# First projection section in contraction order, last pair's down weights in two parts, seventeen weight buffers in a diffusion transformer block

## The chip, the core and the metric

The kernel runs on one core of a Trainium2 chip. The metric is the device time of one execution in microseconds (us). Engines are named as in the profile: PE (TensorE, matrix products), DVE (VectorE), ACT (ScalarE), POOL (GpSimd) and SP (SyncE, which here only issues transfers). Before the change three executions took 1332.74, 1338.11 and 1338.48 us, median 1338.11.

## The reference

One block for 512 tokens of width 1024, with 256 context tokens, all in f32. A condition vector gives six vectors of shift, scale and gate (`adaln`). The mixer is a gated linear recurrence with four heads in both directions, started from states of the context, beside a short convolution. The second half is a mixture of 16 experts in which each expert takes its 64 best tokens.

```python
sh1, sc1, g1, sh2, sc2, g2 = adaln(c, w_ada, b_ada)       # silu(c) @ w_ada + b_ada, split in 6
hc = modulate(rms_norm(ctx, norm_mix), csh1, csc1)         # the same from c_ctx
zf_f, zf_b, i_c = split(hc @ w_in[:, 512:2048])
s_f, s_b = hgrn2_context_states(zf_f, zf_b, i_c, ...)
hx = modulate(rms_norm(x, norm_mix), sh1, sc1)
q, zf_f, zf_b, i, g, gate_b, gate_c, v = split(hx @ w_in)  # eight sections of 512 columns
x = x + g1 * (concat(o_hgrn, gate_b * dwconv3(gate_c * v)) @ w_out)
h = modulate(rms_norm(x, norm_ffn), sh2, sc2)
aff = softmax(h @ w_router); gate, idx = top_k(aff.T, 64)
hid = silu(xs @ w_gate) * (xs @ w_up)                      # xs = h[idx], per expert 64 x 1024
x = x + g2 * scatter_add(idx, gate * (hid @ w_down))       # w_*: 16 experts, 1024 x 2048
out = rms_norm(x, norm_final)
```

## The kernel before

**Front.** The first 71 us compute shift and scale of the first norm and section 1 of `w_in` (the forward gates). A unit of `w_ada` is 1024 rows by 256 columns, 1 MB (`ada_unit`, L183): eight products into four column groups of PE, summed by two transposes and a reduction on DVE (`ada_cols`, L193). A loop over `j` (four steps of two of the eight contraction blocks `k`) loads a scale and a shift unit, modulates blocks `2j` and `2j+1` of tokens (`xnT`) and context (`cnT`), each split into a high and a low part, and adds their products for two of the section's four column groups (`products`, L262). Each f32 product is made of three fast ones: high by high, high by low and low by high. `px_f` and `pc_f` are the sums for the 512 tokens and 256 context tokens. The other two groups follow in `project_T(1, 1)`.

Sections 2, 4 and 3 and the four heads' context states (`context_state`, L369, both directions) follow to 185 us. The remaining columns of `w_ada` are multiplied by the condition on DVE meanwhile (`ada_sum`, L529: one multiply and seven multiply-adds of 128x256 per unit, each vector in four units) and summed over partitions on PE (`ada_r`, `ada_c`); the four units for the second gate `g2b` stand in the head stage among sections 6, 7, 0 and 5 (`sections`, L623). The router's weights `wr` are loaded by POOL after `g2b`'s bias and scaled on DVE (L615). This tile lies in memory that held the context's activations. The head stage ends at 311 us; output projection, router and the choice of tokens fill the time to about 390 us.

**Experts.** Pairs of experts are worked through: gate and up weights in 1 MB tiles (8 KB rows) into four sums `gu` (L897), transposes, and the down product `y` (L954). `scatter` (L927) brings the rows back to their tokens by a product with a 0/1 matrix. SP issues all weight loads in program order into a ring of 4 + 12 buffers (`NA`, `NB`), through `stream` (L60) at line 64. A load waits until the buffer's previous tile has been used.

**Last pair.** The down product of the last two experts goes by column parts 0 to 512, 512 to 768 and 768 to 1024. Each part is finished (L977: gate, scatter, squares for the final norm) while the next one is multiplied; tiles of the last part come in pieces of 256 KB. After the last part each of the four token blocks has its own chain of square, sum, reciprocal root, scaling and output transfer.

The order within an engine is set by a scheduler that follows program order and priorities (`high_priority`), as far as operands and banks allow.

## Time and profile before

| | us |
|---|---|
| three executions | 1332.74, 1338.11, 1338.48 |
| profiled execution, its own time | 1336.76 |
| its span, first to last instruction | 1334.8 |
| first section, to the first `ada_r` product | 0 to 71.4 |
| sections 2, 4, 3 and context states | to 185 |
| head stage | to 311 |
| projection, router, choice of tokens | to about 390 |
| experts | to 1281 |
| last down product and end | to 1334.8 |

The profile is of one execution. PE's clock granted over the span is 0.983 of full speed. A timeline row gives start, duration, engine, line, operation, output and inputs, and in brackets the idle time before it with what ended it. Matmuls overlap their neighbours, so the distance of two starts is the pace, not the duration. SPq is the queue of SP's transfers.

### The profile page before, as it was taken

Reading aid. Unit: us, or ns where it says so; the run is one execution under the profiler, and the core shown is the slowest. Engines: PE = TensorE matmul, PEld = TensorE weight load, DVE = VectorE, ACT = ScalarE, POOL = GpSimd, SP = SyncE. Lnnn points to the kernel's source line nnn. Section 1 sums busy time; section 2 is a strip of 40 time slices with the busy share of each in tenths; the row PEclk is TensorE's granted clock in tenths of the full one; section 3 lists DMA queues with packets and bytes.
Section 4 is the critical chain, followed back from the end, with each engine's and each line's share of the span. In section 5 each row is a group of like instructions: output and inputs, shape, how many; then the busy total and the mean of one; then the engine's idle time right before and its main releaser. Section 6 shows DMA issues by size and latency. Waiting matters only on the chain.

```text
span 1334.8 us, 15459 instructions
## 1 busy us (share of the span) xinstructions
PE 1264.9 (95%) x6374; PEld 692.5 (52%) x6374; DVE 420.5 (32%) x969; ACT 245.0 (18%) x494; POOL 43.6 (3%) x51
## 2 busy tenths in 40 slices
PE   5999989998969999999999999999999999999996
PEld 3788978776844443444444344344434434443433
DVE  5776467986451112112101211211021121102114
ACT  5633444334211200010000001000000100000002
POOL 1000022140000000000000000000000000000000
PEclk9999989998979999999999999999999999999998
DMA  9868223316389989999999999999999999999996
GB/s 328 267 201 261 96 82 96 127 64 234 143 330 407 358 347 426 426 427 427 427 426 426 425 427 427 427 427 426 425 427 427 427 427 426 427 425 427 426 385 215
DMA packets 112082, 458.85 MB, mean 344 GB/s; under 512 B 7310, under 2 KB 56571, under 8 KB 64907
## 3 DMA queue, kind: packets, MB, share of 16 engines
q1 hardware_dynamic: 110832, 454.06, 84.6%
q0 software_dynamic: 992, 3.74, 0.8%
q8 instruction: 50, 0.82, 0.2%
q14 instruction: 22, 0.17, 0.0%
q10 hardware_dynamic: 186, 0.06, 0.0%
HBM read 455.73 MB, written 2.10 MB: 343 GB/s over the span
## 4 chain that ended last, share of the span: by engine, by line
PE 87%; DVE 7%; ACT 3%; DMA 2%; issue 1%; POOL 0%; DVEq 0%; ACTq 0%; POOLq 0%; SPq 0%
PE gu L897 37%; PE y L954 17%; PE pg L855 5%; PE po L929 3%; PE px L265 3%; PE px L266 3%; PE px L270 3%; PE ht L912 2%; PE y L1009 1%; PE wo L710 1%; PE wo L711 1%; PE wo L712 1%; DMA wd<-in_w_down 1%; PE pi L335 1%; PE pi L333 1%
## 5 line engine op out<-in xcount | busy, mean ns | idle before, releaser
L897 PE MATMUL gu<-wg,xs 128*64 128x512 f32 x1024 | 461.7, 599 | 0.7 <-ACT gs L907 0.7
L897 PE MATMUL gu<-wu,xs 128*64 128x512 f32 x1024 | 460.7, 599 | 0.0
L954 PE MATMUL y<-wd,hid 128*64 128x512 f32 x896 | 239.2, 598 | 0.0
L897 PEld LDWEIGHTS gu<-wg,xs 128*64 128x64 f32 x1024 | 128.7, 136 | 158.1 <-issue 154.3
L897 PEld LDWEIGHTS gu<-wu,xs 128*64 128x64 f32 x1024 | 128.7, 136 | 123.1 <-issue 122.5
L907 DVE COPY gs<-gu 128x512 f32<-128x512 f32 x32 | 22.0, 691 | 389.8 <-PE gu L897 389.8
L954 PEld LDWEIGHTS y<-wd,hid 128*64 128x64 f32 x896 | 82.2, 136 | 120.1 <-issue 113.8
L907 ACT COPY gs<-gu 128x512 f32<-128x512 f32 x32 | 18.7, 587 | 455.1 <-PE gu L897 455.1
L265 PE MATMUL px<-h_hi,whi 128*128 128x512 f32 x208 | 85.1, 409 | 0.0
L270 PE MATMUL px<-h_hi,wlo 128*128 128x512 f32 x208 | 84.0, 404 | 0.0
L855 PEld LDWEIGHTS pg<-ohr,x 128*128 128x128 f32 x512 | 62.4, 195 | 40.6 <-issue 38.9
L266 PE MATMUL px<-h_lo,whi 128*128 128x512 f32 x208 | 83.4, 401 | 0.0
L855 PE MATMUL pg<-ohr,x 128*128 128x128 f32 x512 | 71.8, 289 | 1.5 <-DVE ohr L847 1.5
L861 DVE TENSOR_SCALAR xs<-pg,a,b 128x128 f32<-128x128 f32 x32 | 13.1, 410 | 149.1 <-PE pg L855 149.1
L258 DVE TENSOR_TENSOR wlo<-wi,whi 128x1024 fp32r<-128x1024 f32 x32 | 42.3, 1326 | 34.4 <-ACT whi L257 34.3
L923 DVE SCALAR_TENSOR_TENSOR yt<-y,gate,g2b 128x512 f32<-128x512 f32 (+1 forms) x17 | 12.2, 719 | 128.8 <-PE y L954 108.6
L535 DVE SCALAR_TENSOR_TENSOR adas<-wa,cs,adas 128x256 f32<-128x256 f32 x112 | 51.5, 492 | 1.2
L858 ACT ACTIVATE xs<-pg,b,a 128x128 f32<-128x128 f32 x32 | 14.6, 457 | 199.7 <-PE pg L855 199.7
L929 PE MATMUL po<-yhl,g 128*128 128x512 f32 (+1 forms) x136 | 41.7, 418 | 7.5 <-ACT yhl L924 7.0
L265 PEld LDWEIGHTS px<-h_hi,whi 128*128 128x128 f32 x208 | 40.2, 193 | 8.4 <-issue 0.4
L966 DVE TENSOR_TENSOR acc<-acc,po 128x512 f32<-128x512 f32 x56 | 36.0, 684 | 26.8 <-PE po L929 26.8
L929 PEld LDWEIGHTS po<-yhl,g 128*128 128x128 f32 x136 | 22.4, 189 | 42.1 <-ACT yhl L924 14.3
...
## 6 DMA issues: line engine op xcount, KB each, us to landing
wg<-in_w_gate SPq DMA_DIRECT2D x128, 1024.0 KB, 17.4
wu<-in_w_up SPq DMA_DIRECT2D x128, 1024.0 KB, 18.1
wd<-in_w_down SPq DMA_DIRECT2D x124, 1024.0 KB, 19.5
...
```

The source lines that it names most:

```text
L258: dve.tensor_tensor(lo, v, hi.bitcast(F32), op=ALU.subtract)
L265: mm(px, hi[:, k], h_hi[:, k], start=f, stop=False)
L266: mm(px, hi[:, k], h_lo[:, k], start=False, stop=False)
L270: mm(px, lo[:, k], h_hi[:, k], start=False, stop=l)
L535: dve.scalar_tensor_tensor(acc, t[:, k * 256:(k + 1) * 256], cs[:, k, 0:1], acc, op0=ALU.mult, op1=ALU.add)
L855: mm(pg[:, :P], x1[:, tb, k * P:(k + 1) * P], ohr[:, tb], start=tb == 0, stop=tb == NT - 1)
L897: mm(gu[n][i * CAP:(i + 1) * CAP], xs[:, k, ssl], w[:, n * 512:(n + 1) * 512], start=k == 0, stop=k == KD - 1, skip_group_check=True)
L907: (act.copy if n % 2 else dve.tensor_copy)(to, fr)
L912: pe.transpose(pt[:, i * P:(i + 1) * P], gs[:, f * P:(f + 1) * P], ident)
L929: mm(po, g[:, tb * P:(tb + 1) * P], yhl[:, i, nsl], start=first and i == 0, stop=i == 1)
L954: mm(y[n][i * CAP:(i + 1) * CAP], hid[:, i, f], wd[i][:, s, n * 512:(n + 1) * 512], start=f == 0, stop=f == DFF // P - 1, skip_group_check ...
L966: dve.tensor_tensor(acc[tb][:, nsl], acc[tb][:, nsl], po, op=ALU.add)
```

## The change

The ring of buffers in `ring_b` grows from 12 to 13. Memory for it comes from sharing: one tile (`shared`) holds the small constants and later the experts' gathered tokens `xs`, and one (`pool_a`) the working rows of the top-k and later the one-hot `ohr`.

The first section is computed for all four column groups at once, in order of the contraction: `k` 0 to 3 for the tokens, then for the context, then `k` 4 to 7. `w_ada`'s units become 512 wide (two tiles of 1 MB, rows of 2 KB), four instead of eight; `w_in`'s section comes in two halves of rows. Column sums become four products with a 128x2 matrix `sel`. The context is loaded after the first half of the weights.

The later `w_ada` units are 512 wide too, eight instead of sixteen, each with its product one unit later. All of `g2b`'s are done before the head stage, and its bias is loaded early. The last pair's down product goes by two halves of 512 columns; its last tiles come in pieces of 512 KB; the first half's finish stands one tile later in its part; one reciprocal root serves all four token blocks, and ACT scales all four first halves.

```diff
-NB = 12
+NB = 13
...
-    for src, name in ((cx_r, "xt_c"), (x_r[:, 0:2], "xt_0"), (x_r[:, 2:4], "xt_1")):
+    for src, name in ((x_r[:, 0:2], "xt_0"), (x_r[:, 2:4], "xt_1"), (cx_r, "xt_c")):
         t = early.tile([P, 2048], F32, name=name)
-        sp.dma_start(out=t.rearrange("p (a b) -> p a b", a=2), in_=src)
+        if name != "xt_c":
+            sp.dma_start(out=t.rearrange("p (a b) -> p a b", a=2), in_=src)
         xt.append(t)
+    xt = xt[2:] + xt[:2]
...
+    shared = const.tile([P, KD * P], F32, name="shared")
+    ones = shared[:, :CTX]
...
-    def ada_unit(col0, t):
-        pa = bank("kv" if (col0 // 1024) % 2 else "o", 1, f"ada_{col0}")
+    def ada_loads(col0):
+        return [stream(wa_r[:, 4 * q:4 * q + 4, col0:col0 + 512], f"wa_{col0}_{q}")
+                for q in range(2)]
+    def ada_unit(col0, ts):
+        pa = bank("o", 1, f"ada_{col0}")
         for k in range(KD):
             g = k % 4
-            mm(pa[32 * g:32 * g + 32, :256], cs[:, k, :], t[:, k * 256:(k + 1) * 256],
+            mm(pa[32 * g:32 * g + 32], cs[:, k, :], ts[k // 4][:, g * 512:(g + 1) * 512],
                start=k < 4, stop=k >= 4, skip_group_check=True)
-        ev = early.tile([P, 256], F32, tag="adaev", name=f"ada_ev_{col0}", bufs=2)
-        act.copy(ev, pa[:, :256])
+        ev = early.tile([P, 512], F32, tag="adaev", name=f"ada_ev_{col0}", bufs=1)
+        act.copy(ev, pa)
...
+        for b in range(4):
+            mm(pt[:, 2 * b:2 * b + 2], ev[:, b * P:(b + 1) * P], sel, start=b == 0, stop=b == 3,
+               skip_group_check=True)
+        dve.tensor_tensor(dst, pt[:, 0:8].rearrange("p (b m) -> p b m", b=4),
+                          bias.unsqueeze(2).to_broadcast([P, 4, 2]), op=ALU.add)
...
+    def first_products(k, ctx_too):
+        hi, lo = (t[:, k % 2] for t in first_w[k // 2])
+        for i in range(4):
+            f, l, bs = k == 0, k == KD - 1, slice(i * P, (i + 1) * P)
+            if ctx_too:
+                pc = first_c[i // 2][:, (i % 2) * CTX:(i % 2 + 1) * CTX]
+                mm(pc, hi[:, bs], hc_hi[:, k], start=f and i % 2 == 0, stop=False,
+                   skip_group_check=True)
+                mm(pc, hi[:, bs], hc_lo[:, k], start=False, stop=False, skip_group_check=True)
+                mm(pc, lo[:, bs], hc_hi[:, k], start=False, stop=l, skip_group_check=True)
+            else:
+                mm(first_x[i], hi[:, bs], h_hi[:, k], start=f, stop=False)
+                mm(first_x[i], hi[:, bs], h_lo[:, k], start=False, stop=False)
+                mm(first_x[i], lo[:, bs], h_hi[:, k], start=False, stop=l)
...
+    wsc, wsh = [ada_loads(D)], [ada_loads(0)]
+    first_raw = lambda i: stream(wi_r[:, 4 * i:4 * i + 4, 512:1024], f"wi_1_{i}")
+    raws = [first_raw(0)]
+    sp.dma_start(out=xt[0].rearrange("p (a b) -> p a b", a=2), in_=cx_r)
+    for i in range(2):
+        rms_rows(xt[1 + i], f"x{i}")
+    with tc.high_priority(offset=PRIO):
+        modulation(0)
+    transpose_x()
+    wsc.append(ada_loads(D + 512))
+    wsh.append(ada_loads(512))
+    raws.append(first_raw(1))
+    for j in range(2):
+        ks = range(4 * j, 4 * j + 4)
+        for n in (2 * j, 2 * j + 1):
+            first_parts(n)
+            for k in (2 * n, 2 * n + 1):
+                modulate(xnT, h_hi, h_lo, k, 0)
...
+        for k in ks:
+            first_products(k, False)
         if j == 0:
             rms_rows(xt[0], "c")
             transpose_ctx()
-            for i in range(2):
-                rms_rows(xt[1 + i], f"x{i}")
-            transpose_x()
-        for k in (2 * j, 2 * j + 1):
-            for src, hi, lo, m in ((xnT, h_hi, h_lo, 0), (cnT, hc_hi, hc_lo, 1)):
-                sca, sft = a1[:, k, m:m + 1], b1[:, k, m:m + 1]
-                act.activation(hi[:, k], src[:, k], AF.Identity, scale=sca, bias=sft)
-                dve.tensor_scalar(src[:, k], src[:, k], sca, sft, op0=ALU.mult, op1=ALU.add)
-                dve.tensor_tensor(lo[:, k], src[:, k], hi[:, k].bitcast(F32), op=ALU.subtract)
-        if first is None:
-            parts = split_w(1, 0)
-            first = [(bank("mm", 4, f"px_f{i}"), bank("mm", 4, f"pc_f{i}")) + parts[i]
-                     for i in range(2)]
-        for px, pc, hi, lo in first:
-            products(px, pc, hi, lo, (2 * j, 2 * j + 1))
+        for k in ks:
+            modulate(cnT, hc_hi, hc_lo, k, 1)
+            first_products(k, True)
+        if j == 0:
+            with tc.high_priority(offset=80):
+                modulation(1)
...
-        t = stream(wa_r[:, :, col0:col0 + 256], f"wa_{col0}")
-        acc = p_sig.tile([P, 256], F32, tag="adas", name=f"adas_{col0}", bufs=2)
-        dve.tensor_scalar(acc, t[:, :256], cs[:, 0, 0:1], None, op0=ALU.mult)
+        ts = ada_loads(col0)
+        acc = p_c.tile([P, 512], F32, tag="adas", name=f"adas_{col0}", bufs=2)
+        dve.tensor_scalar(acc, ts[0][:, :512], cs[:, 0, 0:1], None, op0=ALU.mult)
         for k in range(1, KD):
-            dve.scalar_tensor_tensor(acc, t[:, k * 256:(k + 1) * 256], cs[:, k, 0:1], acc,
-                                     op0=ALU.mult, op1=ALU.add)
+            dve.scalar_tensor_tensor(acc, ts[k // 4][:, (k % 4) * 512:(k % 4 + 1) * 512],
+                                     cs[:, k, 0:1], acc, op0=ALU.mult, op1=ALU.add)
...
+    g2b = const.tile([P, D], F32, name="g2b")
+    tc.keep_in_program_order(gp.dma_start(out=g2b, in_=bass.AP(
+        tensor=b_ada.tensor, offset=b_ada.offset + 5 * D, ap=[[0, P], [1, D]])))
...
+        for i, dst in ((3, b2), (4, a2), (2, g1b), (5, g2b)):
+            for j in range(2):
+                col0 = i * D + 512 * j
+                acc = ada_sum(col0)
+                if last:
+                    last()
+                if i == 3:
+                    last = lambda a=acc, c=col0, j=j: more_cols(a, c, b2[:, 4 * j:4 * j + 4])
+                elif i == 4:
+                    last = lambda a=acc, c=col0, j=j: more_scale(a, c, a2[:, 4 * j:4 * j + 4],
+                                                                 col("nffn", 4 * j, 4))
+                else:
+                    last = lambda a=acc, c=col0, j=j, d=dst: more_rows(a, c, d[:, 512 * j:512 * j + 512])
+                yield
...
+        for _ in project_T(2, half, *keep_sig(1)):
+            next(more)
     for half in range(2):
         run(project_T(4, half, keep_g))
-    more_ada(3)
-    tc.keep_in_program_order(act.preload_act_table_set("natural_log_exp_and_others"))
+        next(more)
...
-    g2b = rowb.tile([P, D], F32, name="g2b")
-    gp.dma_start(out=g2b, in_=bass.AP(tensor=b_ada.tensor, offset=b_ada.offset + 5 * D,
-                                      ap=[[0, P], [1, D]]))
...
-                if i < 2:
-                    at = 256 * (2 * half + i)
-                    more_rows(5 * D + at, g2b[:, at:at + 256])
...
-        ohr = fp.tile([P, NT, 2, CAP], F32, tag="ohr", name=f"ohr_{p}", bufs=1)
+        ohr = pool_a[:, :NT * 2 * CAP].rearrange("p (t e s) -> p t e s", t=NT, e=2)
...
-        xs = fp.tile([P, KD, P], F32, tag="xs", name=f"xs_{p}", bufs=1)
+        xs = shared.rearrange("p (k s) -> p k s", k=KD)
...
-    cuts = [(0, 512), (512, 768), (768, 1024)]
+    cuts = [(0, 512), (512, 1024)]
...
+    pos = [bank2("gu", 4, f"po_{p}_{tb}") for tb in range(NT)]
+    for tb in range(NT):
+        mm(pos[tb], ident, acc[tb][:, 512:], start=True, stop=False)
...
-            if j == 0 and ended:
+            if j == 1 and ended:
...
+    s1 = const.tile([P, NT], F32, name="s1")
+    dve.tensor_tensor(s1, ss[:, :, 0], ss[:, :, 1], op=ALU.add)
+    r4 = rsqrt_mean(s1, D, NT, const, "r3")
     for tb in range(NT):
-        s1 = const.tile([P, 1], F32, tag="ss2", name=f"ss3_{tb}", bufs=2)
-        dve.tensor_reduce(s1, ss[:, tb], op=ALU.add, axis=AX.X)
-        r = rsqrt_mean(s1, D, 1, const, f"r3{tb}")
-        dve.scalar_tensor_tensor(acc[tb][:, nsl], pos[tb][:, :w], r, nf[:, nsl], op0=ALU.mult,
+        r = r4[:, tb:tb + 1]
+        dve.scalar_tensor_tensor(acc[tb][:, nsl], pos[tb], r, nf[:, nsl], op0=ALU.mult,
                                  op1=ALU.mult)
-        if tb % 2 == 0:
-            act.activation(acc[tb][:, :n0], acc[tb][:, :n0], AF.Copy, scale=r)
-        else:
-            dve.tensor_scalar(acc[tb][:, :n0], acc[tb][:, :n0], r, None, op0=ALU.mult)
+        act.activation(acc[tb][:, :n0], acc[tb][:, :n0], AF.Copy, scale=r)
```

**PE, start of section 1.** In the order before, from the first product on (`ada` is a unit of `w_ada`, `ada_t` its transposes; whi and wlo the parts of `w_in`):

```order
L265 MATMUL px_f_326<-h_hi,whi_0_0_318 128x512
L187 MATMUL ada_357<-wa_354,cs 32x256 x8
L266 MATMUL px_f_326<-h_lo,whi_0_0_318 128x512
L268 MATMUL pc_f_327<-hc_hi,whi_0_0_318 128x256
L270 MATMUL px_f_326<-h_hi,wlo_0_0_319 128x512
L265 MATMUL px_f_326<-h_hi,whi_0_0_318 128x512
L197 MATMUL ada_t_368<-ident,ada_ev_366 128x128 x2
L265 MATMUL px_f_328<-h_hi,whi_0_1_322 128x512
L266 MATMUL px_f_328<-h_lo,whi_0_1_322 128x512
L269 MATMUL pc_f_327<-hc_lo,whi_0_0_318 128x256
```

In the changed kernel:

```order
L209 MATMUL ada_t_225<-sel,ada_ev_223 128x2 x4
L310 MATMUL px_f_152<-h_hi,whi_0_288 128x512
L311 MATMUL px_f_152<-h_lo,whi_0_288 128x512
L310 MATMUL px_f_153<-h_hi,whi_0_288 128x512
L311 MATMUL px_f_153<-h_lo,whi_0_288 128x512
L310 MATMUL px_f_154<-h_hi,whi_0_288 128x512
L311 MATMUL px_f_154<-h_lo,whi_0_288 128x512
L312 MATMUL px_f_152<-h_hi,wlo_0_289 128x512
L312 MATMUL px_f_153<-h_hi,wlo_0_289 128x512
```

The products for the context and the next ada units, which stood between those for the tokens, are no longer here; four sums `px_f` take turns on one `k`.

**DVE, last context states.** `wr` is the router's scaling, `pr_c`, `sigc` and `kk_c` the chain of head 3's forward and backward state. Before:

```order
L373 SCALAR_TENSOR_TENSOR pr_c_1702<-ones,sigc_3_711 128x256
L379 TENSOR_TENSOR kk_c_1699<-kk_c_1699,sigc_3_711 128x256
L615 TENSOR_TENSOR wr_1761<-wr,a_585 128x128
L373 SCALAR_TENSOR_TENSOR pr_c_1719<-ones,sigc_3_1039 128x256
L377 TENSOR_TENSOR sigc_3_1039<-pr_c_1719,sigc_3_1039 128x256
L533 TENSOR_SCALAR adas_2334<-wa_2332,cs 128x256
L379 TENSOR_TENSOR kk_c_1716<-kk_c_1716,sigc_3_1039 128x256
```

In the changed kernel:

```order
L429 SCALAR_TENSOR_TENSOR pr_c_1594<-shared,sigc_3_646 128x256
L599 TENSOR_TENSOR g2b<-g2b,ada_r_1626 128x512
L683 TENSOR_TENSOR wr_1654<-wr,a_630 128x128
L435 TENSOR_TENSOR kk_c_1591<-kk_c_1591,sigc_3_646 128x256
L429 SCALAR_TENSOR_TENSOR pr_c_1611<-shared,sigc_3_933 128x256
L433 TENSOR_TENSOR sigc_3_933<-pr_c_1611,sigc_3_933 128x256
L435 TENSOR_TENSOR kk_c_1608<-kk_c_1608,sigc_3_933 128x256
```

The router's scaling has moved ahead of the last step of the forward state, and `g2b`'s last sum stands in front of it.

**PE, last down product.** `y` is the running part, `po` a finished part's scatter, wd_2_1 the last tiles of the three parts and wd_1_3 those of the two. Before:

```order
L1009 MATMUL y_2_7474<-wd_2_0_7475,hid_7146 64x256
L1009 MATMUL y_2_7474<-wd_2_0_7476,hid_7146 64x256
L929 MATMUL po_0_1_7505<-yhl_7342,g_7202 128x256 x2
L929 MATMUL po_1_1_7512<-yhl_7342,g_7202 128x256 x2
L1009 MATMUL y_2_7474<-wd_2_1_7533,hid_7146 64x256
L929 MATMUL po_2_1_7519<-yhl_7342,g_7202 128x256 x2
L1009 MATMUL y_2_7474<-wd_2_1_7534,hid_7146 64x256
L1009 MATMUL y_2_7474<-wd_2_1_7533,hid_7146 64x256
L929 MATMUL po_3_1_7526<-yhl_7342,g_7202 128x256 x2
```

In the changed kernel the first half's scatters and the tiles behind them:

```order
L995 MATMUL po_2_0_7268<-yhl_7162,g_7022 128x512 x2
L995 MATMUL po_3_0_7275<-yhl_7162,g_7022 128x512
L1078 MATMUL y_1_7221<-wd_1_1_7236,hid_6966 64x512
L995 MATMUL po_3_0_7275<-yhl_7162,g_7022 128x512
L1078 MATMUL y_1_7221<-wd_1_1_7237,hid_6966 64x512
L1078 MATMUL y_1_7221<-wd_1_1_7236,hid_6966 64x512
```

The finish of the part before now stands ahead of the second of four tile pairs of the last part, and no longer among the last pair's products.

More of the change, by code (lines that the diff above doesn't have):

```diff
@@ L275, in dit_block @@
     b1 = const.tile([P, KD, 2], F32, name="b1")
-    first = None
-    for j in range(4):
-        ksl = slice(2 * j, 2 * j + 2)
-        wsc, wsh = (stream(wa_r[:, :, at:at + 256], f"wa_{at}") for at in (D + 256 * j, 256 * j))
-        with tc.high_priority(offset=PRIO if j else 0):
-            ada_scale(ada_unit(D + 256 * j, wsc), D + 256 * j, a1[:, ksl], col("nmix", 2 * j, 2))
-            ada_cols(ada_unit(256 * j, wsh), 256 * j, b1[:, ksl])
+    first_x = [bank("mm", 4, f"px_f{i}") for i in range(4)]
@@ new lines, in first_parts, with modulation @@
+    def first_parts(n):
+        hi, lo = (p_h.tile([P, 2, 512], F32R, tag="whl", name=f"w{q}_1_{n}", bufs=6)
+                  for q in ("hi", "lo"))
+        v = raws[n // 2].rearrange("p (k n) -> p k n", k=4)[:, 2 * (n % 2):2 * (n % 2) + 2]
+        act.copy(hi, v)
+        dve.tensor_tensor(lo, v, hi.bitcast(F32), op=ALU.subtract)
+        first_w[n] = hi, lo
+    def modulation(j):
+        ksl = slice(4 * j, 4 * j + 4)
+        ada_scale(ada_unit(D + 512 * j, wsc[j]), j, a1[:, ksl], col("nmix", 4 * j, 4))
+        ada_shift(ada_unit(512 * j, wsh[j]), j, b1[:, ksl])
@@ L586, in dit_block @@
     for half in range(2):
         project_i(half)
+        next(more)
         for h in (2 * half, 2 * half + 1):
@@ L590, in dit_block @@
                 context_state(d, h)
+    run(more)
     p_c.release()
@@ L1010, in dit_block @@
                            start=f == 0, stop=f == DFF // P - 1, skip_group_check=True)
-            if j == 0 and ended:
+            if j == 1 and ended:
                 finish(*ended)
         ended = c, y, nsl
-        if c == 0:
-            pos = [bank2("gu", 4, f"po_{p}_{tb}") for tb in range(NT)]
-            for tb in range(NT):
-                mm(pos[tb][:, :D - cuts[last][0]], ident, acc[tb][:, cuts[last][0]:], start=True,
-                   stop=False)
     o_r = out[0].rearrange("(a p) d -> p a d", p=P)
```

96 lines of the change are left out of this document (48 added, 48 removed).

## The prediction

> **What bounds the kernel now.** I read the shares and the slices first.
>
> ```profile
> PE 1264.9 (95%) x6374; PEld 692.5 (52%) x6374; DVE 420.5 (32%) x969; ACT 245.0 (18%) x494; POOL 43.6 (3%) x51
> PE   5999989998969999999999999999999999999996
> DMA  9868223316389989999999999999999999999996
> ```
>
> TensorE is nearly always busy, and from the tenth slice on the DMA engines are too; in the first slice both are short of work or data. The table by stretches tells which of the two is late where (columns: stretch in us, PE, PEld, DVE, ACT, POOL busy with counts, granted clock, DMA share, GB/s).
>
> ```profile
> 0.00:24.00 24.00, 10.04 (x69) 7.03 (x69) 10.40 (x48) 11.86 (x23) 3.98 (x13) 1.00 0.97 317
> 24.00:71.40 47.40, 45.62 (x316) 34.68 (x317) 32.80 (x79) 28.41 (x44) 0.00 (x0) 1.00 0.88 281
> 71.40:177.00 105.60, 105.60 (x680) 94.99 (x678) 65.08 (x140) 41.95 (x76) 1.45 (x2) 1.00 0.56 179
> 182.30:192.50 10.20, 10.20 (x36) 8.85 (x35) 7.39 (x17) 6.06 (x11) 4.75 (x5) 0.50 0.34 105
> 243.70:247.10 3.40, 3.40 (x10) 2.62 (x9) 3.40 (x9) 0.44 (x1) 0.00 (x0) 0.50 0.02 5
> 247.10:311.00 63.90, 62.23 (x440) 51.75 (x438) 52.44 (x93) 20.61 (x55) 19.64 (x15) 1.00 0.26 86
> 362.00:497.00 135.00, 121.36 (x619) 61.37 (x620) 32.80 (x124) 21.58 (x50) 0.00 (x0) 0.95 0.90 359
> 497.00:1259.00 762.00, 751.14 (x3342) 325.66 (x3339) 122.20 (x264) 58.88 (x123) 0.54 (x1) 1.00 1.01 427
> 1259.00:1302.00 43.00, 39.43 (x157) 16.17 (x154) 5.04 (x9) 3.32 (x7) 0.00 (x0) 1.00 1.03 394
> ```
>
> Up to 24 us the loads decide (DMA 0.97, PE 10 of 24 us). From 24 to 177 us PE does. From 497 us to the end of the stream DMA is saturated at 427 GB/s, so the last byte of weights lands at a fixed distance after 497 us, whatever PE does; PE lives on the buffers filled ahead. Between 362 and 497 us DMA is only 0.90 busy: some 13 us in which it waits for a free buffer, as its queue's waits say.
>
> ```profile
> SPq L64 <- PE gu L897: 209.0, 114, 18.1
> SPq L64 <- PE y L954: 126.1, 45, 8.1
> ```
>
> At the end the lead is used up. The chain that ended last runs through PE, then a load, then PE again, and the matmul concerned shows the wait.
>
> ```profile
> 1277.85 0.63 PE po L1017 x2
> 1281.20 13.75 DMA wd<-in_w_down
> 1295.09 3.67 PE y L1009 x15
> ...
> 1315.67 0.67 PE po L929 x4
> ...
> 1318.38 3.18 PE y L1009 x26
> ```
>
> PE idles 3.6 of the 43 us from 1259 us (row above): that much at least it is behind because of loads. So two things move the end: how early the whole of the front part is done (it shifts PE's consumption and, through freed buffers, the DMA), and the DMA stream itself.
>
> **Terms.** All against the profiled execution (1336.76 us, span 1334.8); the median of the runs, 1338.11, lies 1.35 us above it.
>
> *First section, start.* Its first product and the first instruction behind it:
>
> ```profile
> 26.56 0.49 PE L265 MATMUL px_f<-h_hi,whi 128*128 128x512 f32 x1 [0.58 <-ACT whi L257]
> 71.41 0.59 PE L543 MATMUL ada_r<-adas,ones 128*128 128x256 f32 x2
> ```
>
> After the change 7 MB of 1.05 million bytes each stand ahead of this product (two of x, four of w_ada, one of w_in). At the 317 GB/s of the first stretch they land by 23.2 us. At the 366 GB/s of a stretch in which 2 KB rows are loaded (the row 1284 to 1297 below) it is 20.1 us, and w_ada's rows grow from 1 to 2 KB. Column sums, modulation and split add 2 to 4 us, as some 2 us of it can lie under the w_in load. That gives 22 to 27 us; I take 24: **-2.5 us** (-4.5 to +0.5).
>
> *First section, the rest.* Before it takes 71.41 - 26.56 = 44.85 us. The number of products is unchanged: 4 column groups x 8 steps x 3 = 96 of 512 columns and 96 of 256. Their pace shows in neighbours elsewhere:
>
> ```profile
> 171.07 0.39 PE L265 MATMUL px<-h_hi,whi 128*128 128x512 f32 x1
> 171.29 0.39 PE L266 MATMUL px<-h_lo,whi 128*128 128x512 f32 x1
> 169.44 0.28 PE L333 MATMUL pi<-whi,hc_hi 128*128 128x256 f32 x1
> 169.56 0.28 PE L334 MATMUL pi<-wlo,hc_hi 128*128 128x256 f32 x1
> ```
>
> That is 0.22 to 0.23 and 0.12 us, together some 33.3 us. About 11.5 us of the 44.85 are thus ada units, column sums and waits. After the change half of the ada work (four 256-wide equivalents of eight) lies behind the first product where six lay before; the context's 16 transposes move behind it, at about the same price. So PE's own work is nearly equal, and what can go is waiting: PE's products of steps 0 to 3 (48 x 0.23 = 11 us, then 5.7 us for the context) cover the second half of the loads. By 24 + 11 + 6 + 4 = 45 us all thirteen megabytes are there even at 317 GB/s (43 us). Waiting in the old order is at most the 11.5 us less six ada units; I estimate 4 us, of which 2 return in the chain from the column sums through one bank: **-2.5 us** (-4.5 to +2).
>
> *From 71 to 177 us* PE has neither gap nor slack (105.60 of 105.60 us busy), and DVE has 40 us free. The column work there is the same, in half as many pieces of twice the width; the second vector's four units (16 us of DVE by the row below, a quarter less when 512 wide, by the 0.75 us of such a form further down) come into this stretch. I cost it at nothing: DVE's free 40 us hide it. If that cover is gone, PE waits for DVE and up to 4 us are lost.
>
> ```profile
> L535 DVE SCALAR_TENSOR_TENSOR adas<-wa,cs,adas 128x256 f32<-128x256 f32 x112 | 51.5, 492 | 1.2
> ```
>
> *The router's weights.* They are loaded into memory that the context's activations hold until the last `pi` product, and DVE's scaling of them (L615) stands in order ahead of the chain for the last context state:
>
> ```profile
> 170.88 0.55 POOL L610 DMA_DIRECT2D g2b<-in_b_ada  x1 [150.85 <-PE pt_c L382]
> 171.42 0.92 POOL L613 DMA_DIRECT2D wr<-in_w_router  x1
> 178.78 0.29 DVE L615 TENSOR_TENSOR wr<-wr,a 128x128 f32<-128x128 f32 x1 [4.04 <-DMA wr<-in_w_router]
> 181.19 0.41 PE L382 MATMUL pt_c<-ident,kk_c 128*128 128x128 f32 x2 [3.98 <-DVE kk_c L379]
> ```
>
> The load takes 7.3 us, PE stops for 4 us, and 10.2 us at half clock follow (row 182.30 above), which cost 5 more. In the new order g2b's 512 KB no longer go ahead of it, so the load starts 0.5 us earlier and may land as early as 5 us after its issue; but the scaling moves one context state forward (second order excerpt above), so two states wait behind it instead of one. Product end to scaling becomes 5.5 to 8 us; PE has about 4 us of other work in between; then 0.3 and 0.4 us to the first state, some 2 us to the second. Stall 2 to 6 us against 4: **0** (-3 to +4, with the clock).
>
> *Head stage, 192 to 311 us.* DVE is the busiest engine beside PE (52 of the 63.9 us from 247), and PE loses about 1.7 us in the last row of the table and 2.1 us here:
>
> ```profile
> 242.63 0.94 PE L456 MATMUL kv<-vtok,kT 128*128 128x128 f32 x6 [2.10 <-ACT kT L443]
> ```
>
> with 3.4 us at half clock behind it (1.7 more). The four units of the second vector leave DVE's list here, 4 x 8 x 0.49 = 16 us. Most of that time lies beside PE's own work; at most the 5.5 us come back: **-1.5 us** (-5 to 0).
>
> *One more weight buffer.* While a load waits for a buffer ahead of 497 us, a seventeenth lets one more megabyte go: 1.05 MB / 427 GB/s = 2.45 us. The stream never stops afterwards, so it ends that much earlier, and PE, at least 3.6 us behind for it, can follow: **-2.45 us** (0 if the buffers are held by something else).
>
> *Last pair, loads.* The two quarters of the last 8.4 million bytes come in 1 KB rows, the half before in 2 KB rows:
>
> ```profile
> 1284.00:1297.00 13.00, 11.26 (x54) 3.88 (x52) 0.00 (x0) 0.00 (x0) 0.00 (x0) 1.00 1.02 366
> 1302.50:1316.50 14.00, 14.00 (x103) 8.36 (x103) 5.39 (x11) 2.93 (x9) 0.00 (x0) 0.90 0.97 331
> ```
>
> 8.4 MB at 331 and at 366 GB/s are 25.3 and 22.9 us; per unit of DMA share (341 and 359) 24.6 and 23.4. **-1.3 us** (-2.4 to -1.2).
>
> *Last pair, end.* Behind the last landing (last issue 1311.4, 5.5 us to land: 1317) PE has 3.4 us of scatter and y left, because the second quarter's finish stands in front (chain, 1315.67 to 1318.38). Now the first half's finish stands two tiles earlier (third order excerpt), and y can end 1 to 1.5 us after the last landing: -3. Against that the last part is 512 wide and one rsqrt waits for all four squares.
>
> ```profile
> L923 DVE SCALAR_TENSOR_TENSOR yt<-y,gate,g2b 128x512 f32<-128x512 f32 x1 | 0.8, 751 | 16.8 <-PE y L1009 16.8
> L925 DVE TENSOR_TENSOR yhl<-yt,yhl 128x512 fp32r<-128x512 f32 x1 | 0.7, 693 | 0.7 <-ACT yhl L924 0.7
> L1026 ACT ACTIVATE junk_l<-po 128x256 f32<-128x256 f32 x4 | 1.5, 383 | 1.0 <-PE po L929 1.0
> 1327.23 3.36 SPq L1037 DMA_DIRECT2D out<-acc  x4
> ```
>
> Before, 5.7 us lie between the last y product (1321.5) and the first output transfer. After: 0.75 for yt, some 0.6 for the cast, 0.69, 0.3 for a scatter, four squares at about 0.8 with their reads (3.2), 1.3 for the rsqrt's steps, 0.9 for scaling and issue: 7.7 to 8.6, so +2 to +2.9. The four transfers follow as before. **-0.5 us** (-1 to +1).
>
> Sum: -2.5 - 2.5 + 0 + 0 - 1.5 - 2.45 - 1.3 - 0.5 = -10.75. Set against the median that is 1327.4; I round to **1328 us**, -0.75%.
>
> **A rule beside it.** Half clock comes in the trace in stretches of 3.4 us (243.70) and 10.2 us (182.30), three times as much; the first follows a stop of PE of only 2.1 us. Each 3.4 us of it cost 1.7. So moving the same stall against these stretches is worth steps of 1.7 us, with nothing else changed.
>
> [...]
>
> **Rivals.**
> 1. *The front's gain is eaten before the experts* (chance 0.22). The chain of the second half's column sums (four context tiles and two sums take turns in one bank) and the router's wait with two states behind it take back 4 to 6 us. For it: DVE's order, and 10.2 us of half clock hang on this spot. Against it: the router's load is freed of g2b. 1331.5 to 1335; within 0.5%.
> 2. *The head stage gives all that DVE is spared, or the clock's stretches fall well* (0.12): -14 to -17, 1321 to 1324. Against: its stops name ACT, not DVE.
> 3. *The extra buffer brings nothing* (0.06), because the DMA's 13 idle us come from issues that wait for semaphores rather than buffers: 1330.5.
> 4. *The other side: loads come too late for the second half of the contraction* (0.12). PE's first half ends by 24 + 17 + 4 = 45 us; if the thirteenth megabyte lands after that, PE stops and cools. 1 KB rows and waits made the first 24 us 317 GB/s; if the second halves' issues wait for freed buffers at the ada products, at 200 GB/s the last lands at 68 us, PE waits 23 us and, with the 11 + 6 us of products left, the section ends at 85 instead of 67 us: some 1346. It decides from 45 us on. Against it: DMA is 0.97 busy there already, so it isn't the issue that limits.
>
> **Chances.** Forecast 0.48, with its own range 1323 to 1331. A difference of 0.5% (6.7 us) is about what a measurement of this kernel can tell from none: faster means below 1331.4, slower above 1344.8. Faster: 0.44 of the forecast, rival 2, half of rival 3: 0.59. Same: the rest of the forecast, rival 1, half of rival 3 and 0.02 of rival 4: 0.31. Slower: 0.10. The range 1320 to 1338 takes in rivals 1 to 3 and leaves out rival 4 and some 0.05 beyond rival 2.
>
> **What would show it.** First product at 24 us and the first `ada_r` at 66 to 67 us instead of 71.4; one stall at the router's weights of 2 to 6 us; DMA share from 362 to 497 us up by about 0.02; the wait at the last pair's first down product unchanged or shorter, and y's last product at once behind the last landing; 7.7 to 8.6 us from there to the first output. Wrong would be: gaps of PE between 24 and 67 us, a longer half-clock stretch behind the router's wait, or an unchanged idle DMA between 362 and 497 us.

## The result, and the profile after

| | before | after |
|---|---|---|
| median (lowest to highest), us | 1335.55 (1332.74 to 1338.48), 4 runs | 1350.07 (1348.93 to 1352.37), 4 runs |
| profiled execution: time, span, us | 1336.76, 1334.8 | 1348.93, 1347.1 |
| first product of the first section (`px_f`) | 26.56 | 27.82 |
| first instruction behind the first section | 71.41 | 80.03 |
| first `wo` product | 317.07 | 316.30 |
| first and last `gu` product (experts) | 394.12, 1277.26 | 392.72, 1288.05 |
| first output transfer | 1327.23 | 1339.01 |

The change made the kernel slower: ratio after to before 1.0125, interval [1.0101, 1.0149], some 14 to 17 us. The table of starts, read from the trace, says where. The front is 8.6 us late after its first section, has more than recovered that by `wo`, and reaches the experts 1.4 us ahead of before. Between the first and the last `gu` product it then takes 895.33 instead of 883.14 us. So the loss lies in a stage in which no instruction of a middle pair was changed.

The page of the changed kernel, engines' shares first, then GB/s in 40 slices:

```profile
PE 1279.8 (95%) x6246; PEld 686.5 (51%) x6246; DVE 405.0 (30%) x847; ACT 236.6 (18%) x477; POOL 43.2 (3%) x48
GB/s 358 205 188 266 202 88 72 63 63 282 153 347 393 354 352 420 420 420 419 420 420 421 420 419 420 420 420 420 420 420 420 420 420 420 419 421 421 419 388 191
```

The shares look as before. The last line holds the news: the plateau stands at 420, where the stretch 497 to 1259 of before showed 427. The stretches (columns as in the prediction):

```profile
0.00:24.00 24.00, 10.77 (x73) 5.63 (x73) 10.00 (x42) 9.36 (x17) 2.64 (x11) 1.00 0.94 347
24.00:80.00 56.00, 53.23 (x264) 37.50 (x265) 32.10 (x61) 25.45 (x39) 1.91 (x3) 0.94 0.61 214
80.00:177.00 97.00, 96.99 (x625) 87.25 (x624) 59.98 (x92) 33.15 (x65) 0.00 (x0) 1.00 0.68 225
186.80:190.20 3.40, 3.40 (x13) 2.82 (x12) 0.56 (x2) 1.03 (x4) 0.00 (x0) 0.50 0.00 0
190.20:310.00 119.80, 118.56 (x840) 99.09 (x838) 96.27 (x169) 49.25 (x108) 36.21 (x31) 1.00 0.23 76
362.00:497.00 135.00, 121.36 (x611) 60.67 (x611) 32.58 (x122) 20.27 (x47) 0.00 (x0) 0.94 0.91 362
497.00:1259.00 762.00, 751.14 (x3298) 325.01 (x3296) 122.15 (x264) 58.88 (x123) 0.54 (x1) 1.00 1.01 420
1259.00:1302.00 43.00, 43.00 (x167) 17.21 (x165) 3.07 (x6) 2.70 (x6) 0.00 (x0) 1.00 1.03 403
```

The DMA share is 1.01 before and after, and PE's busy time from 497 to 1259 us is the same to the hundredth (751.14 us). Only the counts differ, 3298 products instead of 3342. So the time that PE loses to late weights does not show as idle time in its rows; it shows in the count. Split at 970 us, the same view shows when that begins; first before:

```profile
497.00:970.00 473.00, 466.52 (x2082) 203.02 (x2080) 75.18 (x168) 36.24 (x76) 0.00 (x0) 1.00 1.01 427
970.00:1259.00 289.00, 284.62 (x1262) 122.64 (x1259) 47.03 (x96) 22.64 (x47) 0.54 (x1) 1.00 1.01 427
```

and after:

```profile
497.00:970.00 473.00, 466.51 (x2082) 203.12 (x2080) 75.14 (x168) 36.24 (x76) 0.00 (x0) 1.00 1.01 420
970.00:1259.00 289.00, 284.62 (x1218) 121.89 (x1216) 47.01 (x96) 22.65 (x47) 0.54 (x1) 1.00 1.01 420
```

Up to 970 us PE lives on the lead in its buffers and does the same 2082 products. Behind that 44 of 1262 are missing. The waits of the DMA's queue from 497 to 1300 us agree (sum, times, longest); before, SPq waited for `gu` products to free a buffer 135.5 us in 95 waits. After:

```profile
SPq L64 <- DMA wd<-in_w_down: 188.0, 90, 4.5
SPq L64 <- PE gu L963: 77.0, 63, 8.4
SPq L64 <- PE y L1020: 51.0, 25, 7.5
```

PE holds the stream back less than before, and the stream itself is what everything waits for. One megabyte takes 2.4698 us before and 2.5088 after (a line through the landing times from 520 to 1230 us of the 106 to 108 loads whose landing the trace tells, against their place in the queue); over the 820 us from 497 us to before's last landing 1.6% is 13 us.

### The profile page after: what moved, and what is told of

The parts are those of the page before. It is cut to its first block, busy times and chain, and to the rows that moved or that the text cites. A ratio compares the mean times of both kernels' runs of the same rounds, so it can differ in the third digit from the quotient of the medians.

```text
span 1347.1 us, 15053 instructions
## 1 busy us (share of the span) xinstructions
PE 1279.8 (95%) x6246; PEld 686.5 (51%) x6246; DVE 405.0 (30%) x847; ACT 236.6 (18%) x477; POOL 43.2 (3%) x48
## 4 chain that ended last, share of the span: by engine, by line
PE 82%; issue 12%; DVE 3%; ACT 2%; DMA 1%; POOL 0%; POOLq 0%; DVEq 0%; ACTq 0%
PE gu L963 33%; PE y L1020 16%; PE pg L921 5%; PE px L277 3%; PE px L278 3%; PE px L282 3%; PE po L995 2%; PE ht L978 2%; PE wo L776 1%; PE ada L194 1%; PE wo L777 1%; PE wo L778 1%; PE pi L390 1%; PE pi L389 1%; PE pi L388 1%
## 5 line engine op out<-in xcount | busy, mean ns | idle before, releaser
L963 PE MATMUL gu<-wg,shared 128*64 128x512 f32 x1024 | 463.6, 600 | 0.7 <-ACT gs L973 0.7
L963 PE MATMUL gu<-wu,shared 128*64 128x512 f32 x1024 | 462.6, 600 | 0.0
L963 PEld LDWEIGHTS gu<-wg,shared 128*64 128x64 f32 x1024 | 129.0, 137 | 162.9 <-issue 158.4
L963 PEld LDWEIGHTS gu<-wu,shared 128*64 128x64 f32 x1024 | 129.1, 137 | 127.2 <-issue 124.8
L921 PEld LDWEIGHTS pg<-pool_a,x 128*128 128x128 f32 x512 | 62.5, 195 | 40.6 <-issue 38.9
L921 PE MATMUL pg<-pool_a,x 128*128 128x128 f32 x512 | 71.9, 290 | 1.5 <-DVE pool_a L913 1.5
L924 ACT ACTIVATE shared<-pg,b,a 128x128 f32<-128x128 f32 x32 | 14.6, 458 | 201.0 <-PE pg L921 201.0
L995 PE MATMUL po<-yhl,g 128*128 128x512 f32 x128 | 40.4, 427 | 5.9 <-ACT yhl L990 5.9
L591 DVE SCALAR_TENSOR_TENSOR adas<-wa,shared,adas 128x512 f32<-128x512 f32 x56 | 41.4, 748 | 1.5 <-DMA wa<-in_w_ada 0.4
L978 PE MATMUL ht<-ident,gs 128*128 128x128 f32 x256 | 34.9, 279 | 6.9 <-DVE hid L982 6.9
```

Of the source, the lines that this page charges most:

```text
L591: dve.scalar_tensor_tensor(acc, ts[k // 4][:, (k % 4) * 512:(k % 4 + 1) * 512], cs[:, k, 0:1], acc, op0=ALU.mult, op1=ALU.add)
L921: mm(pg[:, :P], x1[:, tb, k * P:(k + 1) * P], ohr[:, tb], start=tb == 0, stop=tb == NT - 1)
L963: mm(gu[n][i * CAP:(i + 1) * CAP], xs[:, k, ssl], w[:, n * 512:(n + 1) * 512], start=k == 0, stop=k == KD - 1, skip_group_check=True)
L978: pe.transpose(pt[:, i * P:(i + 1) * P], gs[:, f * P:(f + 1) * P], ident)
L995: mm(po, g[:, tb * P:(tb + 1) * P], yhl[:, i, nsl], start=first and i == 0, stop=i == 1)
```

## Experiments

Question one is why the same transfers run at 420 instead of 427 GB/s. In that stage the change touched only three things: a thirteenth buffer, the shared places of `xs` and the one-hot `ohr`, and where the buffers lie, since new and shared tiles ahead of the ring moved its start. By the two programs' memory maps, the twelve `ring_b` buffers of before start at multiples of 256 B of a partition's memory, and the four `ring_a` ones at 96 B past a multiple of 256. After, thirteen start 224 B past a multiple of 256 and four at 64. The theory: the address costs 7 GB/s. Rival A: the thirteenth buffer does it (more loads in flight). Rival B: something else of the change loads the DMA engines.

**e10, the transfer by itself.** Loads of 1 MB in rows of 8192 B into 17 buffers, nine times over, with all computation left out. From one series to the next the buffers' address moves, and other experts' weights are read (one execution):

```diff
+    for n, off in enumerate((0, 32, 64, 96, 128, 160, 192, 224, 0)):
+        pool = tc.alloc_tile_pool(name=f"s{n}", bufs=1, side="left")
...
+            pad = pool.tile([P, (BASE + off) // 4], F32, name=f"pad{n}")
...
+        for i in range(40):
+            t = pool.tile([P, 2048], F32, tag=f"w{i % 17}", name=f"at{off}_{n}_{i}")
+            e, k = (5 * n + i // 8) % 16, i % 8
+            sp.dma_start(out=t, in_=w_gate[0, e, k * P:(k + 1) * P, :])
```

> Loads alone: nine stretches of 40 tiles of 1 MB from the gate weights into 17 buffers, whose start lies 0, 32, 64, 96, 128, 160, 192, 224 and again 0 bytes beyond a multiple of 256; all of the block's computation is left out and the output is zero. Theory A, the address alone slows a load: 427 GB/s or more in the first and last stretch and 418 to 421 in all seven between. Rival, it needs PE's reads of the buffers beside it: the same rate in all nine. Rival, only multiples of 64 matter: 64, 128 and 192 as fast as 0.

The stretches inside the nine series, in the order of the list above (columns: stretch, DVE and POOL busy, granted clock, DMA share, GB/s):

```profile
25.00:95.00 70.00, 0.00 (x0) 0.00 (x0) 1.00 1.01 428
128.00:195.00 67.00, 0.00 (x0) 0.00 (x0) 1.00 1.01 420
230.00:300.00 70.00, 0.00 (x0) 0.00 (x0) 1.00 1.01 422
335.00:400.00 65.00, 0.00 (x0) 0.00 (x0) 1.00 1.01 422
437.00:500.00 63.00, 0.00 (x0) 0.00 (x0) 1.00 1.01 422
540.00:605.00 65.00, 0.00 (x0) 0.00 (x0) 1.00 1.01 422
640.00:705.00 65.00, 0.00 (x0) 0.00 (x0) 1.00 1.01 422
745.00:810.00 65.00, 0.00 (x0) 0.00 (x0) 1.00 1.01 420
850.00:915.00 65.00, 0.00 (x0) 0.00 (x0) 1.00 1.01 428
```

With no engine at work, the address sets the rate: 428 at a multiple of 256 B, again 428 in the repeat at the end (with other weights), 420 at 32 and 224 B past it, 422 in between. Theory A had expected 418 to 421 at all seven. From the landing times of 31 loads in each series, 1 MB takes 2.453 us aligned, 2.494 at 32 and 224 (1.7% more), and 2.480 to 2.487 at 64 to 192 (1.1 to 1.4% more). One load each in the series at 32, 128 and 224 landed 0.5 to 0.7 us late, when a single 8192 B transfer took over 0.7 us; these three delays are taken out.

Why an address off a multiple of 256 B costs time, and why it costs more at 32 and 224 (1.7%) than at 64 to 192 (1.1 to 1.4%), no run shows.

**e4, the kernel before with its buffers moved.** Nothing of the change is in it; one constant tile is wider, and the ring starts 32 B later.

```diff
-    eps = const.tile([P, 1], F32, name="eps")
+    eps = const.tile([P, 16], F32, name="eps")[:, :1]
```

> The kernel of before with 32 bytes more ahead of the buffers: 12 buffers at 32 beyond a multiple of 256 bytes and 4 at 128 beyond one, instead of 12 at 0 and 4 at 96. Nothing else differs. Theory A: 420 GB/s instead of 427 and 1350 to 1355 us. Theory B: 427 GB/s and the time of before, 1333 to 1338 us.

1348.64 us, ratio to before 1.0108 [1.0077, 1.0139]. Its stretch from 500 to 950 us:

```profile
500.00:950.00 450.00, 443.50 (x1973) 193.11 (x1970) 72.90 (x159) 35.68 (x75) 0.00 (x0) 1.00 1.01 420
```

The kernel before becomes as slow as the changed one, at the same 420 GB/s, by 32 B of address.

**e1 and e2, the changed kernel with its buffers moved back.** In e1 all 17 start at multiples of 256 B; in e2 the thirteen do, and the four lie at 96 as before.

```diff
-    sel = const.tile([P, 2], F32, name="sel")
+    sel = const.tile([P, 16], F32, name="sel")[:, :2]
...
-    lt = const.tile([P, 3, 8], F32, name="lt")
+    lt = early.tile([P, 3, 8], F32, name="lt")
...
-    rs2 = pers.tile([P, NT], F32, name="rs2")
+    rs2 = pers.tile([P, 28], F32, name="rs2")[:, :NT]
```

(e2 has the first of the three edits alone.)

> The changed kernel with all 17 weight buffers starting at multiples of 256 bytes in their partition (before the edit: 13 at 224 and 4 at 64 beyond such a multiple; in the kernel of before 12 at 0 and 4 at 96). Theory A, the loads' rate depends on the start address of the buffer: 429 to 431 GB/s from 500 to 950 us instead of 420, PE is no longer behind at the end, 1326 to 1331 us. Theory B, the rate fell because of the seventeenth buffer, the shared memory or the order of loads: 420 GB/s as in the changed kernel, 1349 to 1352 us.

> The changed kernel with 32 bytes more ahead of the buffers: 13 buffers at multiples of 256 bytes, 4 at 96 beyond one. Theory A: 13 of 17 aligned, about 427 GB/s as in the kernel of before (12 of 16), 1328 to 1334 us. Theory B: 420 GB/s, 1349 to 1352 us.

e1 1335.27 us, ratio to before 1.0010 [0.9995, 1.0025]; e2 1336.15, 1.0017 [0.9998, 1.0036]. The same stretch of e1:

```profile
500.00:950.00 450.00, 443.51 (x1978) 193.41 (x1976) 73.71 (x163) 35.80 (x75) 0.00 (x0) 1.00 1.01 427
```

The rate is back, and with it the time: last minus first `gu` start is 881.92 and 882.80 us, against 895.33 in the changed kernel. 14 us hang on 32 B of padding. Both take 2 to 4 us more than the upper end of what was expected, and e1's rate is not the expected 429 to 431. The rest of the change, which the forecast had at -10.75 us, is worth nothing that could be measured.

**e3, the changed kernel with twelve buffers**, at the same address (`NB = 12`): rival A's test.

> The changed kernel with 16 buffers at unchanged addresses, none of them aligned. Theory A: 420 GB/s still, and 2.5 us more than the changed kernel, since one megabyte less goes ahead: 1351 to 1355 us. Theory B (the seventeenth buffer): 427 GB/s, 1333 to 1338 us.

1350.83 us, ratio 1.0121 [1.0089, 1.0153], and 2.5074 us per MB:

```profile
500.00:950.00 450.00, 443.51 (x1971) 192.85 (x1969) 72.90 (x159) 35.38 (x74) 0.00 (x0) 1.00 1.01 420
```

Still 420 GB/s: rival A falls.

**e6 and e7, how much of the address counts.** One execution each: thirteen buffers at 64 and four at 160 past a multiple of 256 (e6); seven of the thirteen aligned, six at 32 and the four at 96 (e7).

```diff
-    sel = const.tile([P, 2], F32, name="sel")
+    sel = const.tile([P, 32], F32, name="sel")[:, :2]
```

```diff
+        if tag == "w7":
+            pool.tile([P, 8], F32, tag="gap", name="gap")
```

(e7 on top of e2.)

> The changed kernel with 13 buffers at 64 beyond a multiple of 256 bytes and 4 at 160 beyond one. If only the distance from a multiple of 64 counts: 427 GB/s from 500 to 950 us and a time as e2's. If a multiple of 256 is needed: 420 GB/s and about 1349 us.

> The kernel of e2 with 32 bytes put in the middle of the ring: 7 buffers at multiples of 256, 6 at 32 beyond, 4 at 96 beyond; the tiles outside the ring stay where e2 has them. If each load's own address sets its time: between 420 and 427, about 422 to 424 GB/s. If other tiles that moved with the ring were the cause: 427 GB/s. If one unaligned buffer in flight slows all: 420 GB/s.

e6 1345.89 us, e7 1340.34; the stretch of e6, then that of e7:

```profile
500.00:950.00 450.00, 443.51 (x1979) 193.51 (x1977) 74.18 (x164) 35.78 (x75) 0.00 (x0) 1.00 1.01 421
```

```profile
500.00:950.00 450.00, 443.51 (x1978) 193.42 (x1975) 73.92 (x164) 35.84 (x75) 0.00 (x0) 1.00 1.01 424
```

A multiple of 64 is not enough (421 GB/s in e6), and a ring that is partly aligned lies in between (424 in e7), so each buffer pays for its own address. With e10's prices, weighed by the number of buffers at each address, 1 MB should take 1.4% more in e6 than with all aligned (e1, 2.4688 us), 1.6% more in the changed kernel, 0.9% in e7 and 0.3% in e2. Measured are 1.4% (2.5024), 1.6% (2.5088), 0.6% (2.4841) and 0.03% (2.4695). So the prices add up, except that the four buffers at 96 cost nothing in e2 and, by the missing 0.3%, in e7. Why they are free stays open.

Question two is what became of the forecast's gain. From here on the base is e2, with the address out of the way.

**e5, the second half's column units in one piece.** The second half of the first section has two units of `w_ada`, for the scale and the shift. In the changed kernel the products of the first of them alternate with the context's transposes. PE's timeline after (start, length, instruction; x2 is one product, which the trace counts twice):

```profile
41.41 1.04 PE L194 MATMUL ada<-spare,shared 128*32 128x512 f32 x2
42.39 0.33 PE L240 MATMUL pt_c<-ident,xt_c 128*128 128x128 f32 x1
42.65 1.04 PE L194 MATMUL ada<-spare,shared 128*32 128x512 f32 x2
43.62 0.33 PE L240 MATMUL pt_c<-ident,xt_c 128*128 128x128 f32 x1
...
50.07 1.05 PE L194 MATMUL ada<-wa,shared 128*32 128x512 f32 x2
51.04 0.33 PE L240 MATMUL pt_c<-ident,xt_c 128*128 128x128 f32 x1
```

The unit's eight products take 9.7 us this way, and the stretch of just that time looks healthy, with PE fully busy and no load under way:

```profile
41.40:51.10 9.70, 9.70 (x25) 2.14 (x25) 1.59 (x4) 1.68 (x3) 0.00 (x0) 1.00 0.00 1
```

e5 puts both units ahead of the transposes:

```diff
+            with tc.high_priority(offset=40):
+                modulation(1)
...
-        if j == 0:
-            with tc.high_priority(offset=80):
-                modulation(1)
```

> The kernel of e2 (13 buffers aligned) with the second half's two ada units issued whole, four column groups together, between the products for the tokens, and the context's transposes behind them instead of alternating with single ada products. Theory A, the alternation makes the four column groups run one after another and costs 9.7 us where a whole unit takes 2.1: the last product of section 1 at about 72 us instead of 80, and 7 us less than e2: 1327 to 1331 us. Rival, the time to 310 us is set by DVE and the loads and PE only waits elsewhere: 1334 to 1337 us.

The first unit's two tiles in e5, four products each, from the same view:

```profile
36.04 1.06 PE L194 MATMUL ada<-spare,shared 128*32 128x512 f32 x8
39.53 1.07 PE L194 MATMUL ada<-wa,shared 128*32 128x512 f32 x8
```

Four products together take 1.06 to 1.07 us, as long as one alone (1.04): each is 32 columns wide of the 128 of a transpose (`128*32` and `128*128` in the rows), and here, with nothing between them, the four overlap in time. 1332.00 us, ratio to before 0.9983 [0.9969, 0.9998]; against e2's 1.0017 some 4.5 us less, where 7 were expected. The first section ends 3.8 us earlier (76.21 against 79.98), but only 2.05 are left at `wo` (314.71 against 316.76), since the router's wait is 4.6 us in this run against 3.0. The rest of the expected gain went within the section, part of it to 3.4 us at half clock from 50.7 us on.

**e9, e2 with the first section of before.** The whole of the first section's reordering undone, and everything else of the change kept.

```diff
-    for src, name in ((x_r[:, 0:2], "xt_0"), (x_r[:, 2:4], "xt_1"), (cx_r, "xt_c")):
+    for src, name in ((cx_r, "xt_c"), (x_r[:, 0:2], "xt_0"), (x_r[:, 2:4], "xt_1")):
...
-    def ada_unit(col0, ts):
-        pa = bank("o", 1, f"ada_{col0}")
+    def ada_unit(col0, t):
+        pa = bank("kv" if (col0 // 1024) % 2 else "o", 1, f"ada_{col0}")
...
-    first_x = [bank("mm", 4, f"px_f{i}") for i in range(4)]
-    first_c = [bank(tag, 1, f"pc_f_{tag}") for tag in ("sc", "kv")]
...
```

> The kernel of e2 (13 buffers aligned) with the first section as it was before the change (units of 256 columns, two column groups of section 1 at a time, context loaded first). Theory, the changed first section costs 8 us by itself: section 1 ends at 71 to 73 us instead of 80 and the time is 5 to 8 us less than e2's, 1327 to 1331 us. Rival, what is gained by then is lost in DVE's work up to 310 us: within 2 us of e2.

1325.97 us, ratio to before 0.9935 [0.9913, 0.9958]: faster than both kernels, and 1 us below the expected range. Its first product stands at 26.58 us, and its waits at the router and at `wo` end here:

```profile
178.26 0.41 PE L394 MATMUL pt_c<-ident,kk_c 128*128 128x128 f32 x2 [3.13 <-DVE kk_c L391]
308.39 0.79 PE L733 MATMUL wo<-wo_hi,m 128*128 128x512 f32 x1 [6.15 <-ACT m L693]
```

`wo` starts 8.7 us ahead of before (317.07) and 8.4 ahead of e2; the first `gu` is 9.2 ahead, the last 9.05, and the span 9.7 shorter. So this gain of the front went through to the end in full, as the forecast had it, with the stream at 427 GB/s (500 to 950 us); and the reordering of the first section is a loss of some 8 us (8.15 at the first `gu` and 7.7 in the span against e2).

**e12, e9 with `g2b`'s sums back in the head stage.** In units 256 wide as before, though with one working tile for their sums.

```diff
-        for i, dst in ((3, b2), (4, a2), (2, g1b), (5, g2b)):
+        for i, dst in ((3, b2), (4, a2), (2, g1b)):
...
+                if i < 2:
+                    at = 256 * (2 * half + i)
+                    late_rows(5 * D + at, g2b[:, at:at + 256])
```

> The kernel of e9 with the second gate's sums (four units of 256 columns on DVE, four products on PE) back among the head stage's sections, its bias still loaded early. Theory, it is this work's leaving the head stage that let the stretch from the first section to the output projection shrink by 8.7 us against the kernel of before: 4 to 5 us come back, with a stop of PE and a half-clock stretch between 190 and 300 us; 1330 to 1331 us. Rival, the gain comes from the router's load alone, with no g2b load ahead of it and a shorter half-clock stretch: within 1.5 us of e9, 1325 to 1327.5 us.

1336.97 us, ratio 1.0021 [1.0005, 1.0037], 11 us more than e9 where 4 to 5 were expected. PE's timeline at the two places:

```profile
239.10 0.94 PE L468 MATMUL kv<-vtok,kT 128*128 128x128 f32 x6 [2.07 <-ACT kT L455]
300.90 2.08 PE L488 MATMUL o<-vtok,both 128*128 128x128 f32 x8 [5.10 <-DVE both L485]
```

The first stop is the one of before (2.10 us at 242.63) and is back with the sums. The second one, with 6.8 us at half clock around it, is new, and one working tile instead of two may be its cause; that part of the 11 us is not settled.

**e8 and e11, buffer count and tail, with the address right.** e8 is e2 with `NB = 12`. e11 is e8 with the last pair cut as before (its tile `sel` is padded further, so that the ring stays aligned).

```diff
-    cuts = [(0, 512), (512, 1024)]
+    cuts = [(0, 512), (512, 768), (768, 1024)]
...
-            if j == 1 and ended:
+            if j == 0 and ended:
...
-    r4 = rsqrt_mean(s1, D, NT, const, "r3")
...
+        s1 = const.tile([P, 1], F32, tag="ss2", name=f"ss3_{tb}", bufs=2)
+        dve.tensor_reduce(s1, ss[:, tb], op=ALU.add, axis=AX.X)
+        r = rsqrt_mean(s1, D, 1, const, f"r3{tb}")
```

> The kernel of e2 with 12 instead of 13 buffers in the second ring, 16 in all, same alignment. Theory, one megabyte less goes ahead of the saturated stretch: the stream ends 2.45 us later and the time is 1.5 to 2.5 us more than e2's. Rival, the extra buffer is worth nothing: same time as e2 within 0.5 us.

> The kernel of e8 (12 aligned buffers in the second ring) with the last pair's down product and end as before the change: three parts, 256 KB pieces, four separate reciprocal roots. Theory, the change of the end is worth what the profiles show, 1 to 2 us: 1338 to 1339 us where e8 has 1337. Rival, the one reciprocal root and the wide last part cost as much as the loads gain: the same time within 0.7 us.

e8 1337.06 us, 1.0021 [1.0007, 1.0035] against e2's 1.0017 [0.9998, 1.0036]; e11 1337.60, 1.0027 [1.0015, 1.0039]. Neither the thirteenth buffer nor the new tail can be told from nothing. The traces put sizes to it that are below what the times resolve: from the first to the last `gu` start 882.80 us with thirteen buffers (e2) and 884.33 with twelve (e8), 1.5 us; and from the start of the last `yt` to the first output transfer 8.6 to 8.9 us in the new tail (e8, e2), 5.65 in the old one (e11).

## Why the prediction was wrong, step by step

The forecast was -10.75 us against the profiled execution; its span grew by 12.3. In the trace that is -1.4 us up to the first `gu`, +10.0 from there to the last `y` product, +3.2 to the first output, +0.5 behind it.

- **The DMA stream itself: the step that failed.** It said that DMA "is saturated at 427 GB/s, so the last byte of weights lands at a fixed distance after 497 us, whatever PE does", and the extra buffer's -2.45 us rest on it. The rate was taken as unchanged; it hung on the buffers' addresses, and the change moved them: 420 instead of 427 GB/s, about 13 us. e4 gives nearly the whole loss to the kernel before with 32 B of padding, e2 takes it from the changed one with 32 B, and e10 shows it with no computation at work. None of the rivals held this. Rival 4 (loads too late for the second half of the contraction) had its place between 45 and 85 us; but from 20 to 80 us PE's waits name ScalarE alone (0.8 us for `ada_ev`, 2.7 for `whi`), both before 28 us. That its 1346 us lies near the measured time is chance.
- **First section, the rest: -2.5 forecast, +7.4 measured.** The section takes 52.2 us (27.82 to 80.03) instead of 44.85. The count of products was right, their price was not: PE's own work was taken as nearly equal, with the transposes "at about the same price". But single products of a unit stand between the transposes, and the order excerpt shown with the change ends before them. Eight such pairs take 9.7 us. A transpose between two products takes 0.26 us from start to start in the rows above, and in e5 the unit takes 2.1 us, so by estimate the alternation loses 9.7 - 2.1 - 2.1 = 5.5 us; 6.8 us at half clock from 26.4 us lose another 2.7 (half of the 5.4 us from the first product on). These two are 8.2 of the 9.9 us between forecast and measurement.
- **First section, start: -2.5 forecast, +1.3 measured.** The loads were in time; the chain behind them was longer. The timeline of PE and ScalarE after:

```profile
21.34 1.92 PE L194 MATMUL ada<-wa,shared 128*32 128x512 f32 x16
...
25.31 1.52 ACT L295 ACTIVATE h_hi<-xnT,b,a 128x512 fp32r<-128x512 f32 x2 [1.34 <-DVE b L211]
...
26.74 1.03 ACT L318 CAST whi<-spare 128x1024 fp32r<-128x1024 f32 x1
...
27.82 0.79 PE L310 MATMUL px_f<-h_hi,whi 128*128 128x512 f32 x1 [2.74 <-ACT whi L318]
```

  The last `w_ada` products start at 21.34 us, within the forecast's 20.1 to 23.2 for the loads. From there to the first product it is 6.5 us, not "2 to 4": column sums until 25.3, then ScalarE's two modulated tiles, and only behind them on the same engine the cast of `w_in` that the product needs.
- **71 to 177 us, no change: right.** 96.99 of 97.00 us busy (row 80 to 177).
- **The router's wait: 0 forecast, about -4.6 measured.** The load was issued at 179.26 us, and took 6.0 instead of 7.3 us without `g2b` ahead of it:

```profile
185.24 0.29 DVE L683 TENSOR_TENSOR wr<-wr,a 128x128 f32<-128x128 f32 x1 [2.60 <-DMA wr<-in_w_router]
186.02 0.41 PE L438 MATMUL pt_c<-ident,kk_c 128*128 128x128 f32 x2 [2.78 <-DVE kk_c L435]
```

  PE stops 2.78 instead of 3.98 us (-1.2), and 3.4 us at half clock follow instead of 10.2 (half of 6.8: -3.4). The lower end of the step's bounds was -3. Part of this is luck: behind this wait the half clock lasted 3.4 us in e2, 6.8 in e8, 10.2 before and 13.7 in e4, whose code is that of before but for 32 B of padding.
- **Head stage: -1.5 forecast, about -3.8 measured,** within its bounds: the stop of 2.1 us and its 3.4 us at half clock are gone (row 190 to 310: granted clock 1.00). e9 and e12 bear it out in direction; PE gains what those stops were worth, and DVE's 16 us are not the measure.
- **One more buffer: -2.45 forecast.** With the rate right, 1.5 us in the traces, and nothing that the times resolve (e2, e8).
- **The end: -1.3 and -0.5 forecast.** In e2 the last `y` product ends at 1316.1 us instead of 1321.5, of which 1.05 us come from the earlier first `gu`; the tail behind it gives back 3.2 us (8.9 against 5.7; 7.7 to 8.6 forecast), net -1.1. The four squares with their reads were priced at 3.2 us and take 2.4; the reciprocal root's steps were priced at 1.3 and take 2.3, as the changed kernel's rows show:

```profile
L1090 ACT ACTIVATE junk_l<-po 128x512 f32<-128x512 f32 x4 | 2.3, 597 | 1.6 <-PE po L995 1.6
```

```profile
1335.57 0.16 DVE L1092 TENSOR_TENSOR s<-ss 128x4 f32<-128x4 f32 x1 [3.31 <-ACT junk_l L1090]
1337.88 2.56 ACT L1098 ACTIVATE acc<-acc,r3r 128x512 f32<-128x512 f32 x4 [2.35 <-DVE r3r L132]
```

- **The rule beside it.** It took the half clock in stretches of 3.4 us, at 1.7 us each. All half-clock stretches (granted clock 0.50) of before and after but each run's last, which its end cuts short, are 3.4 us or a multiple: 10.2, 3.4, 6.8, 13.7 and 3.4 before; 6.8 from 26.4 us, 3.4 from 186.80, 6.8 and 17.1 in the changed kernel. In e12 it is 6.8 from 299.5 us. The length of a stop alone did not tell what followed it: the stop of 2.78 us in the changed kernel was followed by 3.4 us at half clock, that of 2.10 us before by 3.4 us too, and the same stop of 2.07 us in e12 by none (granted clock 1.00 from 239 to 245 us). No run shows the 1323 us at the lower end of the forecast's range; the lowest median of a whole kernel is e9's 1325.97 us.

So both steps of the first section were wrong by their sign, and the stream by its rate. The head and router steps gave more than forecast and made good part of the first section's error (first `gu` -1.4 us against -6.5 forecast). Of the 23 us between forecast and measurement the rate makes up 12 to 13.
